# Down projection of a hybrid decoder layer in seven block products, with block sums made in place by POOL and VectorE

## The chip, the cores and the metric

The kernel runs on one core of a Trainium2 chip. The metric is the device time of one execution in microseconds (us). The core's engines run side by side, each through its own queue of instructions in order: TensorE (PE) for matmuls, VectorE (DVE), ScalarE (ACT) and POOL (GpSimd) for elementwise work, and SyncE (SP), whose queue issues most of the DMA transfers here. Semaphores make one engine wait for another. Matmuls write to PSUM, which has eight banks of 128 x 512 float32; everything else lies in SBUF.

## The reference

One layer on 512 tokens of width 1024, all in float32: a mixture of two kinds of attention heads, an output projection onto the residual, then a gated feed-forward part, its down projection onto the residual, and a last RMS norm. Only the end matters here (FFN_HIDDEN is 2816):

```python
def rms_norm(x, g):
    xf = x.astype(jnp.float32)
    y = xf * lax.rsqrt(jnp.mean(xf * xf, axis=-1, keepdims=True) + RMS_EPS)
    return (y * g.astype(jnp.float32)).astype(x.dtype)
...
        h = h + mix @ w_out[layer]
        hn = rms_norm(h, norm2_g[layer])
        h = h + (jax.nn.silu(hn @ w_gate[layer]) * (hn @ w_up[layer])) @ w_down[layer]
    return rms_norm(h, norm_f_g)
```

## The kernel before

A float32 matrix product is made of three matmuls of type float32r: each operand is split into a rounded high part (a copy by ScalarE) and the rest, a low part (a subtraction by VectorE), and high x high, high x low and low x high are added up in PSUM. So every operand costs one ScalarE and one VectorE instruction before TensorE can use it. Line 71 is the helper that copies (`copy`), line 76 the one for two-input operations (`tt`), line 84 the low part in `split`, which attention uses, and lines 95 to 97 (`mm3x`) the three matmuls.

Attention and the output projection fill the first half of the span; there POOL has part of the low parts (line 84) and the scaling of the probabilities (line 337). In the second half the gate and up projections run over 22 blocks (units 0 to 21) of 128 hidden columns each; `first_part`, `second_part` and `third_part` make a unit's seven products and leave its gated hidden block, 128 x 512 (hidden column x token), in `zs[j]`. The normed input lies in X1 (tiles X10, X11) and X2 (X20, X21), high and low parts apart. The last product of a unit (the weight "d", in `third_part`) goes into the same bank A that VectorE has just read for the product before it.

Then comes the down projection, `down_step(k)` for each of 22 row blocks of w_down: SP loads a block (128 x 1024, into a `raw2` tile, six buffers), ScalarE and VectorE split it into an `hl2` tile (three buffers), `split_g` splits the hidden block, and `down` makes 4 token tiles x 2 column halves x 3 matmuls of 512 columns. All eight PSUM banks add up over the 22 blocks. The last four blocks are kept back and done token tile by token tile. As soon as a bank is full, VectorE multiplies it by `nrstd_t` and adds it onto the residual (line 838), which `h1_back` fetched again from DRAM (`h1d`) into `cell(t, c)`; ScalarE squares it with a sum (line 657), `rsqrt` takes the root, and both halves are scaled and stored.

VectorE and ScalarE run `down_step` in the order of the code (`tc.manual_schedule`); all other order, that of TensorE and SP too, is the scheduler's, which may put the first down matmuls between the last gate and up products. A load waits on SP until its buffer is free, and what is behind it on SP waits too.

Of the kernel before, what the change touches and what calls it, by code (L numbers as in the profile page):

```python
# [11 lines left out]
F32 = mybir.dt.float32  # L12
F32R = mybir.dt.float32r
# [3 lines left out]
P = 128  # L17
# [35 lines left out]
def tile_hybrid_layer(ctx: ExitStack, tc: tile.TileContext, xT, w_qk0, w_t, w_av, w_vb, w_o, w_gu, w_d,  # L53
# [605 lines left out]
    def rsqrt(ts, out):  # L659

        v, w, r = nv[:, ts], nt[:, ts], out[:, ts]
        nc.vector.scalar_tensor_tensor(out=v, in0=ss[:, ts, 1], scalar=EPS / 4, in1=ss[:, ts, 0], op0=ALU.add, op1=ALU.add)
        nc.scalar.activation(w, v, AF.Sqrt)
# [78 lines left out]
    def third_part(j, u):  # L742
        y, z = u["y"], zs[j]
        product(u["A"], u["w"]["d"], X2, 4, False)
        tt("v", z[:, :HS], u["A"], y[:, :HS], ALU.mult)
        tt("v", z[:, HS:], z[:, HS:], y[:, HS:], ALU.mult)

    es = []
    for f in range(KT):
# [16 lines left out]
        units[1] = first_part(1)  # L766
    second_norm()
    quads = ["act00", "act01", "act10", "act11"]
    zs = [q[:, i] for tag in quads for q in [act.tile([P, 4, S], F32, name=tag)] for i in range(4)]

    second_part(0, units[0])
    third_part(0, units[0])
    for j in range(1, NJ):
# [7 lines left out]
    GT = [ff.tile([P, n, S], F32R, name=tag, bufs=1) for n, tag in ((4, "X10"), (4, "X11"), (10, "X20"), (10, "X21"))]  # L781
    GH = [GT[0][:, k] for k in range(4)] + [GT[2][:, k] for k in range(10)] + [GT[3][:, k] for k in range(8)]
    GL = [GT[1][:, k] for k in range(4)]
    def w_down(k, w=None):
        raw = raw2()
        nc.sync.dma_start(raw, w_d[k * P:(k + 1) * P, :].rearrange("p (a n) -> p a n", a=2))
        return split2(raw, *ENG["d"], w)

    def split_g(k):
        if k % 4 == 0 and k:  # L790
            q = act.tile([P, 4, S], F32R, name=quads[k // 4 - 1]) if k < 20 else GT[3][:, 8:]
            GL.extend(q[:, i] for i in range(min(4, NJ - k)))
        copy("a", GH[k], zs[k])
        tt("v", GL[k], zs[k], GH[k].bitcast(F32), ALU.subtract)

    def down(ps, t, c, k, w):
        tk = slice(t * P, (t + 1) * P)
        mm3x(ps[c][t], GH[k][:, tk], GL[k][:, tk], w[:, :, c], slice(0, HD), k == 0, k == NJ - 1)

    ps = [[bank(n) for n in ("S", "S", "proj", "proj")], [bank(n) for n in ("PT", "PT", "PT", "O")]]  # L800
    def h1_back(t):
        if t % 2 == 0:
            h1r.append(ff.tile([P, 2, D], F32, name=("X10", "X11")[t // 2], bufs=1))
        nc.sync.dma_start(h1r[t // 2][:, t % 2], h1d[t])

    def cell(t, c):
        return h1r[t // 2][:, t % 2, c * HD:(c + 1) * HD]

    h1r, gf, ws_last, wx = [], [], [], []
    def down_step(k):  # L810
        if k < NJ - LAST:
            w = w_down(k)
        elif k < NJ - 2:
            ws_last.append(w_down(k))
        else:
            if k == NJ - 2:
                wx.append(ff.tile([P, 2, 2, 2, WC], F32R, name="X20", bufs=1))
            ws_last.append(w_down(k, wx[0][:, k - NJ + 2]))
        split_g(k)
        if k < NJ - LAST:  # L820
            for c in range(2):
                for t in range(NT):
                    down(ps, t, c, k, w)
        if k in (1, 2):
            gf.append(ff.tile([P, HD], F32, name="g", bufs=BUFS["g"]))
            nc.sync.dma_start(gf[-1], gf_row[:, (k - 1) * HD:k * HD].to_broadcast([P, HD]))
        if k in (7, 9, 11, 13):
            h1_back((k - 7) // 2)
# [4 lines left out]
    for t in range(NT):  # L833
        for c in range(2):
            for i, k in enumerate(range(NJ - LAST, NJ)):
                down(ps, t, c, k, ws_last[i])
            x = cell(t, c)
            nc.vector.scalar_tensor_tensor(out=x, in0=ps[c][t], scalar=nrstd_t[:, t:t + 1], in1=x, op0=ALU.mult,
                                           op1=ALU.add)
            square(t, c, x)  # L840
            if c == 0:
                tt(ENG["c"], x, x, gf[0], ALU.mult)
        rsqrt(slice(t, t + 1), rstd_t)
# [85 lines left out]
```

## Time and profile before

| | us |
|---|---|
| median of 3 runs (670.36 to 671.63) | 670.62 |
| profiled execution, its own time | 670.29 |
| its span | 668.5 |
| TensorE busy in the span | 641.3 (96%) |
| VectorE busy | 477.3 (71%) |
| ScalarE busy | 352.9 (53%) |
| POOL busy, all of it before 300 us | 144.3 (22%) |
| first down matmul starts | 533.82 |
| last down matmul ends | 661.37 |

The span runs from the first to the last instruction that the profile shows; the time of the execution has a little outside of it. A busy time is a sum over an engine's instructions. An engine with less busy time than span is idle in between, and whether that matters is seen from the chain of waits, which is followed back from the last instruction. Times of the rows are from the start of the span.

### The profile page before, as it was taken

How to read it: one execution, taken by the hardware profiler on the slowest of the kernel's cores; microseconds unless marked ns; L12 is line 12 of the kernel's file. 1: busy time of each engine (PE TensorE's matmuls, PEld its weight loads, DVE VectorE, ACT ScalarE, POOL GpSimd, SP SyncE). 2: the span in 40 equal slices, each digit the busy share in tenths (PEclk: the TensorE clock that was granted, in tenths of full speed). 3: DMA queues.
4: the chain of work that ended last, by engine and by line, in shares of the span. 5: the costliest groups of instructions: out<-in, count | busy, mean ns of one | idle time of the engine just before them, and what ended most of it. 6: DMA issues, size and time to landing. Idle time of an engine off the chain costs nothing.

```text
span 668.5 us, 11164 instructions
## 1 busy us (share of the span) xinstructions
PE 641.3 (96%) x3942; PEld 571.3 (85%) x3942; DVE 477.3 (71%) x994; ACT 352.9 (53%) x745; POOL 144.3 (22%) x184
## 2 busy tenths in 40 slices
PE   9999997999999999987999999999999999999995
PEld 6878887878878887866899999999999988888884
DVE  4458777678787679559899899999998724333355
ACT  5543565345775678558774455545545504222234
POOL 7635842153446645330000000000000000000000
PEclk9999999989999999888899999999999999999998
DMA  6666665446225640063433133323324417222003
GB/s 191 216 177 190 174 176 155 123 140 172 90 95 158 199 150 17 1 206 117 179 128 124 69 111 126 111 95 111 111 96 147 175 58 245 102 94 95 0 2 126
DMA packets 45316, 84.44 MB, mean 126 GB/s; under 512 B 6811, under 2 KB 10139, under 8 KB 45260
## 3 DMA queue, kind: packets, MB, share of 16 engines
q1 hardware_dynamic: 44684, 82.67, 39.1%
q10 hardware_dynamic: 576, 1.05, 0.4%
q8 instruction: 31, 0.51, 0.3%
q14 instruction: 25, 0.20, 0.1%
HBM read 68.45 MB, written 7.64 MB: 114 GB/s over the span
## 4 chain that ended last, share of the span: by engine, by line
PE 78%; DVE 8%; ACT 4%; DMA 4%; issue 3%; SPq 2%; POOL 1%; DVEq 0%; ACTq 0%; POOLq 0%
PE proj L89 8%; PE proj L91 8%; PE proj L90 8%; PE S L90 6%; PE S L89 6%; PE S L91 6%; PE PT L340 3%; PE PT L96 2%; PE PT L95 2%; PE PT L97 2%; PE O L356 2%; PE proj L96 2%; PE proj L95 2%; PE proj L97 2%; PE S L317 2%
## 5 line engine op out<-in xcount | busy, mean ns | idle before, releaser
L76 DVE TENSOR_TENSOR hl<-raw,hl 128x1024 fp32r<-128x1024 f32 x64 | 78.0, 1220 | 61.1 <-ACT hl L71 60.8
L71 ACT CAST hl<-raw 128x1024 fp32r<-128x1024 f32 x64 | 67.3, 1053 | 76.8 <-PE O L97 57.1
L84 POOL TENSOR_TENSOR w_hl<-w_raw,w_hl 128x512 fp32r<-128x512 f32 (+1 forms) x47 | 61.4, 1309 | 61.7 <-ACT w_hl L71 31.5
L71 ACT CAST w_hl<-w_raw 128x512 fp32r<-128x512 f32 (+2 forms) x76 | 43.3, 576 | 58.0 <-PE S L91 18.9
L325 ACT ACTIVATE P<-P,mn 128x512 f32<-128x512 f32 (+1 forms) x96 | 53.5, 559 | 13.3 <-DVE mn L323 13.0
L337 POOL TENSOR_SCALAR P<-P,den 128x512 f32<-128x512 f32 (+1 forms) x96 | 51.4, 554 | 41.4 <-DVE den L329 21.5
L76 DVE TENSOR_TENSOR PTl<-PT,PTh 128x512 fp32r<-128x512 f32 (+2 forms) x96 | 43.7, 482 | 10.2 <-ACT PTh L350 9.9
L323 DVE CUSTOM_DVE_ANT_0 P<-S,T 128x512 f32<-128x512 f32 (+1 forms) x96 | 44.0, 483 | 9.8 <-PE S L318 7.6
L89 PE MATMUL S<-X,hl 128*128 128x256 f32 x176 | 49.9, 284 | 0.7 <-ACT xf L721 0.7
L90 PE MATMUL S<-X,hl 128*128 128x256 f32 x176 | 50.0, 284 | 0.3 <-DVE X L76 0.3
L89 PE MATMUL S<-X,w_hl 128*128 128x256 f32 x176 | 49.7, 284 | 0.5 <-ACT xf L732 0.5
L350 ACT CAST PTh<-PT 128x512 fp32r<-128x512 f32 (+2 forms) x96 | 38.2, 426 | 22.7 <-PE PT L340 18.8
L90 PE MATMUL S<-X,w_hl 128*128 128x256 f32 x176 | 49.8, 283 | 0.0
L91 PE MATMUL S<-X,hl 128*128 128x256 f32 x176 | 49.7, 282 | 0.0
L91 PE MATMUL S<-X,w_hl 128*128 128x256 f32 x176 | 49.7, 283 | 0.0
L89 PE MATMUL proj<-xh,w_hl 128*128 128x512 f32 x112 | 45.6, 408 | 0.5 <-DVE va L282 0.4
L71 ACT CAST w_hl<-raw 128x512 fp32r<-128x512 f32 x45 | 27.3, 619 | 35.5 <-PE S L91 28.3
L90 PE MATMUL proj<-xl,w_hl 128*128 128x512 f32 x112 | 44.7, 399 | 0.0
L91 PE MATMUL proj<-xh,w_hl 128*128 128x512 f32 x112 | 44.6, 398 | 0.0
L84 DVE TENSOR_TENSOR w_hl<-w_raw,w_hl 128x512 fp32r<-128x512 f32 (+1 forms) x37 | 27.4, 747 | 15.7 <-ACT w_hl L71 14.4
L340 PE MATMUL PT<-ident,P 128*128 128x128 f32 x240 | 36.8, 277 | 0.8 <-POOL P L337 0.8
L89 PEld LDWEIGHTS S<-X,hl 128*128 128x128 f32 x176 | 33.9, 193 | 1.1 <-ACT xf L721 1.1
(316 smaller groups left out, 1965.1 us busy)
## 6 DMA issues: line engine op xcount, KB each, us to landing
raw<-in_w_gu_dram SPq DMA_DIRECT2D x46, 256.0 KB, 3.3
raw<-in_w_d_dram SPq DMA_DIRECT2D x22, 512.0 KB, 3.3
w_raw<-in_w_gu_dram SPq DMA_DIRECT2D x42, 256.0 KB, 2.7
w_raw<-in_w_t_dram SPq DMA_DIRECT2D x28, 256.0 KB, 2.8
T<-gd SPq DMA_DIRECT2D x64, 64.0 KB, 1.9
w_raw<-in_w_o_dram SPq DMA_DIRECT2D x16, 256.0 KB, 3.1
w_raw<-in_w_vb_dram SPq DMA_DIRECT2D x16, 140.0 KB, 2.2
Qb<-in_xT_dram SPq DMA_DIRECT2D x8, 256.0 KB, 2.8
```

The lines of the kernel that those rows point to most:

```text
L71: nc.scalar.copy(out, in_)
L76: engines[e].tensor_tensor(out=out, in0=in0, in1=in1, op=op)
L84: engines[lo].tensor_tensor(out=w[:, 1, :n], in0=raw[:, :n], in1=w[:, 0, :n].bitcast(F32), op=ALU.subtract)
L89: nc.tensor.matmul(ps, w[:, 0, sl], xh, start=first, stop=False, skip_group_check=skip)
L90: nc.tensor.matmul(ps, w[:, 0, sl], xl, start=False, stop=False, skip_group_check=skip)
L91: nc.tensor.matmul(ps, w[:, 1, sl], xh, start=False, stop=last, skip_group_check=skip)
L95: nc.tensor.matmul(ps, xh, w[:, 0, sl], start=first, stop=False)
L323: nc.vector.tensor_tensor_reduce(out=pp, in0=sv, in1=T[:, S - w:], op0=ALU.add, op1=ALU.min, scale=1.0, scalar=3e38, accum_out=mn[:, t:t + 1])
L325: nc.scalar.activation(pp, pp, AF.Exp, bias=mn[:, t:t + 1], scale=-1.0, accum_out=den[:, t:t + 1])
L337: nc.gpsimd.tensor_scalar(pp, pp, den[:, t:t + 1], 1.0, op0=ALU.mult, op1=ALU.mult)
L340: nc.tensor.transpose(pv[:, kb * P:(kb + 1) * P], pp[:, kb * P:(kb + 1) * P], ident)
L350: nc.scalar.copy(ov[0], pv)
```

## The change

The hidden activations are seen as a matrix A of 512 tokens x 2816, the weights as a matrix B of 2816 x 1024. Both are cut in two each way: A11, A12 are the first 256 tokens with the first and the second half of the hidden columns, A21, A22 the last 256 tokens; B11 and B12 are the two column halves of w_down's first half of rows, B21 and B22 of the second. A half is 11 row blocks, taken in six steps: five of two blocks and one of a single block. Seven products of such blocks, with sums of blocks as operands, take the place of eight plain ones; a product is 11 row blocks x 2 token tiles x 3 matmuls.

The sums are made in place, a step at a time: s1 to s4 overwrite A11 and A21, t1 to t4 overwrite B11 and B12. POOL makes s1, s4 and t1 to t4, VectorE s2 and s3. They are put into the program three steps ahead of the step that uses them (AHEAD); s1 and s3 go with product 0. The products run one after another. After the third step of the next product, VectorE adds a product's banks onto the residual at the places where its sum is wanted (`evict`), so PSUM keeps adding up from product to product where the same sum goes on. `prepare` splits both operands of a step (tiles xe and xf for the activations, hl2 for the weights), `multiply` makes the matmuls. The order on VectorE, ScalarE, POOL and TensorE is the code's, and SP's as well: B11 into raw2 tiles, B12 into what was X1 and a bit of X2, the residual into X20, B22 into X21, B21 into w_hl tiles, then the gain. Unit 21's last product is moved behind step 0 of the down projection. The last three steps of product 6 are kept back and done one token tile after the other.

```diff
-    third_part(NJ - 1, units[NJ - 1])
...
-    with tc.manual_schedule(engines={mybir.EngineType.DVE, mybir.EngineType.Activation}):
-        for k in range(NJ):
-            down_step(k)
...
+    HJ = NJ // 2
+    PAIRS = [slice(k, min(k + 2, HJ)) for k in range(0, HJ, 2)]
...
+    A11, A12, A21, A22 = [hidden(h, r) for h in range(2) for r in range(2)]
...
+    ps_a, ps_c, ps_b = [[bank(n) for n in tags] for tags in (("PT", "O"), ("S", "S"), ("proj", "proj"))]
...
+    def s1(k):
+        tt("p", A21[k], A21[k], A22[k], ALU.add)
...
+    def s2(k):
+        minus("v", A21[k], A22[k], A11[k])
...
+    def s3(k):
+        minus("v", A11[k], A11[k], A21[k])
...
+    def s4(k):
+        minus("p", A21[k], A12[k], A21[k])
...
+    def t1(k):
+        minus("p", B11[k], B12[k], B11[k])
...
+    def t2(k):
+        minus("p", B11[k], B22[k], B11[k])
...
+    def t3(k):
+        minus("p", B12[k], B22[k], B12[k])
...
+    def t4(k):
+        minus("p", B11[k], B21[k], B11[k])
...
+    def evict(ps, th, c):
...
+        for i in range(2):
+            x = cell(2 * th + i, c)
+            nc.vector.scalar_tensor_tensor(out=x, in0=ps[i], scalar=nrstd_t[:, 2 * th + i:2 * th + i + 1], in1=x,
+                                           op0=ALU.mult, op1=ALU.add)
...
+    products = [
+        (ps_a, A11, B11, True, (), [(ps_a, 0, 0)], []),
+        (ps_c, A21, B11, True, (t1,), [(ps_c, 1, 1)], []),
+        (ps_a, A21, B11, False, (s2, t2), [(ps_a, 0, 1)], []),
+        (ps_c, A21, B22, False, (s4,), [(ps_c, 0, 1)], [(0, 1), (1, 1)]),
+        (ps_a, A11, B12, False, (t3,), [(ps_a, 1, 1)], [(2, 1), (3, 1)]),
+        (ps_b, A12, B21, True, (), [(ps_b, 0, 0)], [(0, 0), (1, 0)]),
+        (ps_a, A22, B11, False, (t4,), [], [])]
+    AHEAD = 3
...
+    def prepare(n, k):
+        a, b = products[n][1][k], products[n][2][k]
+        m = a.shape[1]
+        w = ff.tile([P, 2, 2, WC], F32R, name="hl2", bufs=BUFS["hl2"])
+        gh = ff.tile([P, 2, HS], F32R, name="xe", bufs=BUFS["xe"])
+        gl = ff.tile([P, 2, HS], F32R, name="xf", bufs=BUFS["xf"])
+        copy("a", gh[:, :m], a)
+        minus("v", gl[:, :m], a, gh[:, :m].bitcast(F32))
+        copy("a", w[:, 0, :m], b)
+        minus("v", w[:, 1, :m], b, w[:, 0, :m].bitcast(F32))
+        return gh, gl, w
...
+            parts = prepare(n, k)
+            if x == 2:
+                gated(NJ - 1, units[NJ - 1])
+            if n == 0:
+                s3(k)
+                s1(k)
+            if x + AHEAD < len(steps):
+                m, kk = steps[x + AHEAD]
+                for f in products[m][4]:
+                    f(kk)
...
+            if x == 0:
+                last_product(NJ - 1, units[NJ - 1])
+            if n and k == 2:
+                for e in products[n - 1][5]:
+                    evict(*e)
```

POOL's queue ended with the output projection, long before this part (act are hidden tiles of the attention, mf its output):

```order
L337 TENSOR_SCALAR P<-P,den 128x128
L337 TENSOR_SCALAR P<-P,den 128x256
L372 TENSOR_TENSOR act_446<-mf,act_444 128x512
L84 TENSOR_TENSOR w_hl<-w_raw,w_hl 128x512 x3
L925 UNCONDITIONAL_BRANCH
L925 ISA
```

Now it goes on from there. This is the stretch from the third of s1 to the third of t2 (act and h1t hold the hidden blocks, raw_6445 to raw_6450 B11, X_6462 to X_6464 B12, X_6465 B22; a sum over a pair of row blocks of activations is 128x2x256, of weights 128x1024):

```order
L75 TENSOR_TENSOR act_3771<-act_3771,h1t 128x2x256 x2
L75 TENSOR_TENSOR raw_6445<-X_6462,raw_6445 128x1024
L75 TENSOR_TENSOR act_3772<-act_3772,h1t 128x2x256
L75 TENSOR_TENSOR raw_6446<-X_6462,raw_6446 128x1024
L75 TENSOR_TENSOR act_3772<-act_3772 128x256
L75 TENSOR_TENSOR raw_6447<-X_6463,raw_6447 128x1024
L75 TENSOR_TENSOR raw_6448<-X_6463,raw_6448 128x1024
L75 TENSOR_TENSOR raw_6449<-X_6464,raw_6449 128x1024
L75 TENSOR_TENSOR raw_6450<-raw_6450 128x512
L75 TENSOR_TENSOR raw_6445<-X_6465,raw_6445 128x1024
L75 TENSOR_TENSOR raw_6446<-X_6465,raw_6446 128x1024
L75 TENSOR_TENSOR raw_6447<-X_6465,raw_6447 128x1024
```

36 sums follow the output projection where nothing stood. VectorE had two operations a row block in this part, the low part of the weights (hl) and of the hidden block (here act_6598, the high part in X_6453):

```order
L76 TENSOR_TENSOR hl_6595<-raw_6593,hl_6595 128x1024
L76 TENSOR_TENSOR act_6598<-act_3771,X_6453 128x512
L76 TENSOR_TENSOR hl_6627<-raw_6625,hl_6627 128x1024
L76 TENSOR_TENSOR act_6598<-act_3771,X_6453 128x512
L76 TENSOR_TENSOR hl_6658<-raw_6656,hl_6658 128x1024
L76 TENSOR_TENSOR act_6598<-act_3771,X_6453 128x512
```

Now, in product 1, from its third step to its fifth (xf is the low part of the activations, hl that of the weights, X_6464 holds the residual, act_3770 at the left is s2):

```order
L75 TENSOR_TENSOR xf<-act_3771,xe 128x512
L75 TENSOR_TENSOR hl_6695<-raw_6447,hl_6695 128x1024
L867 SCALAR_TENSOR_TENSOR X_6464<-PT,nrstd_t,X_6464 128x512
L867 SCALAR_TENSOR_TENSOR X_6464<-O,nrstd_t,X_6464 128x512
L75 TENSOR_TENSOR xf<-act_3771,xe 128x512
L75 TENSOR_TENSOR hl_6717<-raw_6448,hl_6717 128x1024
L75 TENSOR_TENSOR act_3770<-act_3773,act_3770 128x2x256
L75 TENSOR_TENSOR xf<-act_3772,xe 128x512
L75 TENSOR_TENSOR hl_6738<-raw_6449,hl_6738 128x1024
```

Two low parts a step are left, on weights of half the width and two row blocks; between them now stand the adds onto the residual (line 867) and s2.

## Rows read from the trace of the kernel before

**Rows 1.** The page: busy us, share of the span, instructions of each engine.

```profile
PE 641.3 (96%) x3942; PEld 571.3 (85%) x3942; DVE 477.3 (71%) x994; ACT 352.9 (53%) x745; POOL 144.3 (22%) x184
```

**Rows 2.** By stage: length, busy us (count) PE PEld DVE ACT POOL, PEclk, DMA.

```profile
560.00:580.00 20.00, 20.00 (x88) 16.19 (x87) 6.86 (x8) 6.27 (x8) 0.00 (x0) 1.00 0.55 193
620.00:640.00 20.00, 20.00 (x87) 16.19 (x87) 8.96 (x10) 7.64 (x10) 0.00 (x0) 1.00 0.00 0
```

**Rows 3.** TensorE's first down matmul, then the chain of waits: start, us, what.

```profile
533.82 0.40 PE L95 MATMUL proj<-hl,X 128*128 128x512 f32 x1
...
556.04 0.70 PE PT L95 x3
...
661.13 0.25 PE O L97
...
661.40 0.76 DVE X L838
```

**Rows 4.** Groups by form, 555 to 650 us: busy us, mean ns, idle before.

```profile
L76 DVE TENSOR_TENSOR hl<-raw,hl 128x1024 fp32r<-128x1024 f32 x16 | 19.6, 1225 | 52.9 <-ACT hl L71 52.8
...
L71 ACT CAST hl<-raw 128x1024 fp32r<-128x1024 f32 x15 | 15.8, 1052 | 57.1 <-PE O L97 57.1
...
L76 DVE TENSOR_TENSOR act<-act,X 128x512 fp32r<-128x512 f32 x12 | 8.2, 684 | 0.0
...
L71 ACT CAST X<-act 128x512 fp32r<-128x512 f32 x11 | 6.8, 614 | 0.0
```

**Rows 5.** Order in time on VectorE: start us, us, line, operation, tiles.

```profile
530.13 0.42 DVE L76 TENSOR_TENSOR g<-PT,xf 128x256 f32<-128x256 f32 x1 [0.54 <-ACT xf L721]
...
539.00 0.42 DVE L76 TENSOR_TENSOR h1t<-S,xf 128x256 f32<-128x256 f32 x1 [1.35 <-PE S L91]
```

**Rows 6.** Order in time on SP: the first loads of w_down.

```profile
509.68 20.26 SPq L786 DMA_DIRECT2D raw<-in_w_d_dram  x7
```

**Rows 7.** Order in time on POOL: two sums without company.

```profile
132.44 1.28 POOL L84 TENSOR_TENSOR w_hl<-w_raw,w_hl 128x512 fp32r<-128x512 f32 x1 [5.69 <-ACT w_hl L71]
133.82 0.61 POOL L462 TENSOR_TENSOR cy<-cy,cmn 128x256 f32<-128x256 f32 x1
```

**Rows 8.** The same form on POOL and VectorE side by side, then VectorE alone.

```profile
144.12 1.46 POOL L84 TENSOR_TENSOR w_hl<-w_raw,w_hl 128x512 fp32r<-128x512 f32 x1
...
144.47 1.66 DVE L84 TENSOR_TENSOR w_hl<-w_raw,w_hl 128x512 fp32r<-128x512 f32 x1
...
158.59 0.69 DVE L84 TENSOR_TENSOR w_hl<-w_raw,w_hl 128x512 fp32r<-128x512 f32 x1
```

**Rows 9.** Four VectorE additions beside three POOL sums, and means by form.

```profile
63.69 1.60 POOL L84 TENSOR_TENSOR w_hl<-w_raw,w_hl 128x512 fp32r<-128x512 f32 x1 [1.08 <-PE proj L402]
66.18 3.19 POOL L84 TENSOR_TENSOR w_hl<-w_raw,w_hl 128x512 fp32r<-128x512 f32 x2 [0.89 <-ACT w_hl L71]
...
63.47 4.74 DVE L387 TENSOR_TENSOR Qb<-pf,pos_sb 64x512 f32<-64x512 f32 x4
...
L387 DVE TENSOR_TENSOR Qb<-pf,pos_sb 64x496 f32<-64x496 f32 x2 | 3.3, 1666 | 0.0
L387 DVE TENSOR_TENSOR Qb<-pf,pos_sb 64x512 f32<-64x512 f32 x2 | 1.4, 682 | 0.0
```

**Rows 10.** A VectorE operation on PSUM under a POOL sum.

```profile
160.44 1.30 POOL L84 TENSOR_TENSOR w_hl<-w_raw,w_hl 128x512 fp32r<-128x512 f32 x1 [2.86 <-PE PT L340]
...
160.62 0.69 DVE L76 TENSOR_TENSOR PTl<-PT,PTh 128x512 fp32r<-128x512 f32 x1 [0.32 <-ACT PTh L350]
```

**Rows 11.** Stretches of 1 us, TensorE alone: busy us (count), PEclk, DMA.

```profile
112.00:113.00 1.00, 0.00 (x0) 1.00 0.38 126
113.00:114.00 1.00, 0.04 (x1) 1.00 0.54 143
...
115.00:116.00 1.00, 1.00 (x3) 0.50 0.39 119
...
118.00:119.00 1.00, 1.00 (x6) 1.00 0.51 170
```

More of the change, by code (lines that the diff above doesn't have):

```diff
@@ L34 @@
 RB = 32
-LAST = 4
 DELAY = 3
@@ L777, in tile_hybrid_layer @@
         second_part(j, units[j])
-    third_part(NJ - 1, units[NJ - 1])
[L781 to L804, printed above, removed]
-    def cell(t, c):
[L807 to L828, printed above, removed]
@@ new lines, in tile_hybrid_layer, with hidden, load_w @@
+    PAIRS = [slice(k, min(k + 2, HJ)) for k in range(0, HJ, 2)]
+    def hidden(half, rows):
+        v = []
+        for k in PAIRS:
+            j = k.start + (NJ - 10 if k.start < 10 else 1) * rows
+            v.append(zq[min(j // 4, 4)][:, j - 4 * min(j // 4, 4):][:, :k.stop - k.start, half * HS:(half + 1) * HS])
+        return v
+    A11, A12, A21, A22 = [hidden(h, r) for h in range(2) for r in range(2)]
+    def load_w(dst, kh, ch):
+        for n, k in enumerate(PAIRS):
+            for i in range(k.stop - k.start):
+                r = k.start + i + ((NJ - 10 if k.start < 10 else 1) if kh else 0)
+                nc.sync.dma_start(dst[n][:, i], w_d[r * P:(r + 1) * P, ch * HD:(ch + 1) * HD])
@@ new lines, in minus @@
+    def minus(e, out, in0, in1):
+        tt(e, out, in0, in1, ALU.subtract)
+    ps_a, ps_c, ps_b = [[bank(n) for n in tags] for tags in (("PT", "O"), ("S", "S"), ("proj", "proj"))]
+    def cell(t, c):
+        return x0[2][:, 2 * t + c]
+    with tc.manual_schedule(engines={mybir.EngineType.SP}):
+        r11 = [raw2() for _ in PAIRS]
+        B11 = r11[:5] + [r11[5][:, 0:1]]
+        load_w(B11, 0, 0)
+        x0 = [ff.tile([P, n, WC], F32, name=tag, bufs=1)
+              for n, tag in ((4, "X10"), (4, "X11"), (10, "X20"), (10, "X21"))]
+        B12 = [x0[k // 2][:, 2 * (k % 2):2 * (k % 2) + 2] for k in range(4)] + [x0[2][:, 8:10], r11[5][:, 1:2]]
+        load_w(B12, 0, 1)
+        for t in range(NT):
+            nc.sync.dma_start(x0[2][:, 2 * t:2 * t + 2], h1d[t].rearrange("p (c n) -> p c n", c=2))
+        B22 = [x0[3][:, 2 * k:2 * k + 2] for k in range(5)] + [raw1()[:, None]]
+        load_w(B22, 1, 1)
+        B21 = [ws.tile([P, 2, WC], F32, name="w_hl", bufs=BUFS["w_hl"]) for _ in range(5)] + [raw1()[:, None]]
+        load_w(B21, 1, 0)
+        gf = [ff.tile([P, HD], F32, name="g", bufs=BUFS["g"]) for _ in range(2)]
+        for c in range(2):
+            nc.sync.dma_start(gf[c], gf_row[:, c * HD:(c + 1) * HD].to_broadcast([P, HD]))
@@ new lines, in tile_hybrid_layer @@
+    AHEAD = 3
+    steps = [(n, k) for n in range(7) for k in range(len(PAIRS))]
+    def prepare(n, k):
[9 more added lines that the diff above has]
+        return gh, gl, w
@@ new lines, in multiply @@
+    def multiply(n, i, k, gh, gl, w):
+        ps, first = products[n][0], products[n][3]
+        s = slice(i * P, (i + 1) * P)
+        for j in range(PAIRS[k].stop - PAIRS[k].start):
+            start, stop = first and k == 0 and j == 0, PAIRS[k].start + j == HJ - 1
+            nc.tensor.matmul(ps[i], gh[:, j, s], w[:, 0, j], start=start, stop=False, skip_group_check=True)
+            nc.tensor.matmul(ps[i], gh[:, j, s], w[:, 1, j], start=False, stop=False, skip_group_check=True)
+            nc.tensor.matmul(ps[i], gl[:, j, s], w[:, 0, j], start=False, stop=stop, skip_group_check=True)
@@ new lines, in tile_hybrid_layer @@
+    last = []
+    with tc.manual_schedule(engines={mybir.EngineType.DVE, mybir.EngineType.Activation, mybir.EngineType.Pool,
+                                 mybir.EngineType.PE}):
+        for x, (n, k) in enumerate(steps):
+            if x == len(PAIRS):
+                nc.scalar.activation(nt[:, 0:1], ones[:, 0:1], AF.Sqrt)
+            parts = prepare(n, k)
[8 more added lines that the diff above has]
+                    f(kk)
+            if n == 6 and k >= 3:
+                last.append((k, *parts))
+            else:
+                for i in range(2):
+                    multiply(n, i, k, *parts)
+            if x == 0:
[3 more added lines that the diff above has]
+                    evict(*e)
+            if n and k == 3:
+                for c in products[n - 1][6]:
+                    close(*c)
@@ new lines, in final @@
+    def final(i):
+        x = cell(2 + i, 0)
+        nc.vector.scalar_tensor_tensor(out=x, in0=ps_a[i], scalar=nrstd_t[:, 2 + i:3 + i], in1=x, op0=ALU.mult,
+                                       op1=ALU.add)
+    r2, r3 = slice(2, 3), slice(3, 4)
+    with tc.manual_schedule(engines={mybir.EngineType.DVE, mybir.EngineType.Activation, mybir.EngineType.PE}):
+        root(slice(0, 2))
+        unroot(slice(0, 2))
+        for t in range(2):
+            scale(t)
+            store(t)
+        for x in last:
+            multiply(6, 0, *x)
+        final(0)
+        close(2, 0)
+        root(r2)
+        for x in last:
+            multiply(6, 1, *x)
+        unroot(r2)
+        scale(2)
+        final(1)
+        square(3, 0, cell(3, 0))
+        store(2)
+        root(r3)
+        gain(3)
+        unroot(r3)
+        scale(3)
+        store(3)
```

47 lines of the change are left out of this document (27 added, 20 removed).

## The prediction

> **What bounds the kernel now.** I read the engines' busy times first, then a table by stage, then the chain of waits, then single instructions where engines meet. TensorE is busy for 96% of the span, VectorE for 71%, POOL for 22% [rows 1]. The stage that the change rewrites begins with the first down matmul at 533.82, in between the last gate and up matmuls, and its last matmul ends at 661.37, where the chain passes to VectorE [rows 3]. The table says which engine is short there: TensorE 20.00 of 20.00 us at granted clock 1.00, VectorE 6.86 to 8.96, ScalarE 6.27 to 7.64, POOL nothing [rows 2]. So here a matmul saved is time saved, as long as the other engines keep up. Three matmuls take 0.70 in the chain, 0.233 each [rows 3]. 22 row blocks of 24 matmuls are 528, or 123.2 us; of the 127.55 us from 533.82 to 661.37 the other 4.35 are gate and up matmuls. After TensorE come 7.1 us of closing work up to the end of the span at 668.5, and the profiled execution took 670.29, so 1.8 us lie outside the span; its time is 0.33 under the median of 670.62, less than the runs differ.
>
> **TensorE's share of the change.** Seven products of 11 row blocks, 2 token tiles and 3 matmuls are 462, which is 66 fewer: 66 x 0.233 = 15.4 us. A full step (two row blocks) has 12 matmuls, 2.80 us, the sixth step of a product 1.40, a product 15.4. The last gate and up product now stands between steps 0 and 1 with nothing to fill its wait for VectorE's read of the same bank (the add took 0.42 [rows 5]); I take 0.8, between 0 and 1.5. Alone, this gives a TensorE end of 661.4 - 15.4 + 0.8 = 646.8.
>
> **Splits, loads, evictions.** A full step now splits two row blocks of half width and its own activations: ScalarE 0.61 + 1.05, VectorE 0.68 + 1.23 [rows 4], some 1.7 and 1.9 against 2.80. Each is covered if nothing delays it; three weight buffers (hl2) let a split run at most two steps ahead. The 14 adds onto the residual take 0.76 each [rows 3] and come two in a step. The loads are as many bytes as before. B11 goes into the buffers that took the first w_down blocks before, seven of them issued from 509.68 on [rows 6]; the others wait on SP for X1 and X2 to be free, with only loads queued behind, and POOL wants B22 and B21 tens of us later. I cost them at nothing; if a load is late, it is a us or two. The closing chain is the same operations, 7.1 us.
>
> **The sums on POOL.** Before, POOL did nothing in this stage. Now it has 12 activation sums (s1, s4) and 24 weight sums (t1 to t4). Two inputs of 128x512 took 1.28, of 128x256 0.61 [rows 7]; 128x1024 does not occur. Twice 1.28 is 2.56, and 1.28 plus two more steps of 0.67 is 2.62; I take 2.6, bounds 2.45 and 2.75. POOL's total is 4 x (5 x 2.6 + 1.28) = 57.1 and 2 x (5 x 1.28 + 0.61) = 14.0, together 71 us. Alone that would fit beside 107.8 us of matmuls.
>
> **But the two engines exclude each other.** A VectorE split of 128x512, both inputs in SBUF, takes 0.69 when POOL is idle; begun at 144.47 beside a POOL sum of 144.12 to 145.58 it took 1.66 and ended at 146.13, 0.55 after POOL did [rows 8]. So it did not slow down, it stood still. [Rows 9] show who goes next: four VectorE additions in a row, while POOL had three sums to do. Two took 682 ns, two 1666; the four took 4.74, which is 4 x 0.54 + 2 x 1.28 = 4.72, and POOL's sums ended as if each had gone in after one VectorE operation. They take strict turns, each for a whole operation. A VectorE operation with one input in PSUM runs through: 0.69 under a POOL sum [rows 10]. So the residual adds don't take part, and all splits and the sums s2 and s3 do. The Trainium skill has the rule that speaks against this change: SBUF — State Buffer, section Who interferes with whom, says that a VectorE instruction with two SBUF inputs contends with a GpSimd one that reads SBUF, and the later one fully blocks. The trace agrees on that and on its exemption of one SBUF input; without the exemption the 14 adds would put some 10 us more into the shared time, with it nothing.
>
> **The ledger of the shared access.** A VectorE operation holds it for 0.54 (128x512), 1.22 - 0.14 = 1.08 (128x1024) or 0.28 (128x256). The turns make POOL's work and VectorE's add up until POOL's last sum, t4 of step 5. By when does that come? t4 waits behind t3 and s4 in POOL's queue, and s4 overwrites A21 only after product 2's splits have read it. So t3 and t4, 12 sums, fall beside product 3's 12 splits, one for one. VectorE's holds through product 3: 4 products x (5 x 1.62 + 0.82) = 35.7, s2 and s3 2 x 2.98 = 6.0, leftovers of units 20 and 21 1.6, sum 43.3. With POOL's 71 that is 114. It starts near 530.6, when s3 of step 0 can go behind the read of PT at 530.13 [rows 5]; that gives 645, and I add 4 for stretches in which neither can work (VectorE's queue stands behind the last gate and up product until 541.8): 649. Seen by step: a full step of product 3, and most of product 1, has two sums and two splits in turn, 2 x 2.6 + 1.62 = 6.8 us where TensorE needs 2.80. TensorE, the bound before, starves.
>
> After 649 VectorE is alone and TensorE the bound again: 1.4 for product 3's last step and its split, 3 x 15.4 = 46.2 for products 4 to 6, and 2 for refilling the queue of prepared steps: 699. Starving also costs clock: after TensorE had stood still from 112 to 114 the granted clock was 0.50 (1.2 GHz) for some 3 us and then 1.00 again [rows 11]. In a starved step 2 x 2.80 = 5.6 still fits under 6.8, so I add only 2: 701. With 7.1 and 1.8 the time is **710 us**, 6% slower.
>
> **Rivals.**
> *The sums do not collide (faster).* If POOL's sums found the gaps in VectorE's queue, or these forms did not exclude each other, TensorE would end at 646.8 plus 1 for the tight last steps, and the time is 647.8 + 7.1 + 1.8 = 657. For it: POOL's results are wanted late, and VectorE has some 1 us free per step. Against: that gap is shorter than one sum of 2.6, and every meeting of such a pair in rows 8 and 9 shows the wait. It decides if a split beside a sum takes under about 1.6. With half-collisions up to 669.
> *Exclusive, but better packed.* The shared work in all is 71 + 7 x 8.9 + 6.0 + 5 (gains, stores, leftovers) = 144. If VectorE's late splits could fill every gap, it would end at 530.6 + 144 = 675, with 4 of matmuls, 7.1 and 1.8 behind: 688. Sums of 2.45 in place of 2.6 save 3. For it: turns need not be strict where both are ready at once. Against: hl2's three buffers keep VectorE from splitting ahead of TensorE in products 4 to 6. 688 to 703.
> *The clock stays low.* If TensorE stays at the half level through the starved products, product 2, whose steps have only some 3.8 us of shared work, is paced by 5.6: 5 x 1.8 = 9 more, and a stretch at half level in product 4 costs 2 more: 720. The Trainium skill's TensorE: Matmul & The Clock Gate, section HAM oscillation, tells of a kernel that fell back to the low rate at every step's wait; [rows 11] agree on the fall and show it end after some 3 us. Sums of 2.75 would add 3. 718 to 730.
> *The change does not do what it says*: the order of the instructions has the 462 matmuls in place of 528 and all 36 sums, so no chance is kept for this.
>
> **How the numbers follow.** Turns as computed, 703 to 718: 0.66, since rows 8 to 10 fit to 0.1 us and what is uncertain is the time in which neither works. Better packed: 0.12. Clock or longer sums: 0.11. No collision, or little: 0.10. No difference to be seen: 0.01. A measurement of this kernel tells about 0.2% from no change; by that bound faster is 0.10, same 0.01, slower 0.89. The range reaches to 695 and 724, which takes in both bounds of the 2.6, most of the packed case and half of the clock case.
>
> **What would show it.** In the profile after, POOL's 128x1024 sums should read 3 to 3.7 us rather than 2.6, and VectorE's 128x1024 splits beside them up to 3.7 rather than 1.23; both should fall back to their own times after POOL's last sum, near 649. TensorE should take some 36 us for products 1 and 3, some 20 for product 2, and 15.4 to 16 for products 4 and 5. The time between the last matmul and the end should again be 7 us. The prediction is wrong if VectorE's splits keep 1.23 under POOL's sums (then 657), if POOL has finished before product 2 begins, or if products 4 to 6 are not back at 15.4, in which case something else, a load or the clock, bounds them.

## The result, and the profile after

The changed kernel took 698.16 us (median of 4 runs, 696.08 to 698.63), the kernel before 671.12 in the same comparison: a ratio of 1.0393, interval 1.0362 to 1.0424. It is 27 us slower, where the forecast was 710 with a range of 695 to 724. The profiled execution took 698.63 with a span of 696.8, so again 1.8 us lie outside the span.

The page of the changed kernel, first the busy us of each engine (beside [rows 1]), then the rows of 40 slices, in tenths:

```profile
PE 640.2 (92%) x3876; PEld 565.9 (81%) x3876; DVE 574.3 (82%) x1049; ACT 380.2 (55%) x785; POOL 231.7 (33%) x220
...
PE   8999998899999999888999999999999866867995
...
POOL 6525842345354655200000000000001697797000
PEclk9999998999999999998999999999999988977998
```

TensorE has 66 instructions fewer, VectorE 55 more and POOL 36 more. In the last ten slices TensorE's row falls to 6 to 8 where POOL's row is 6 to 9, and recovers when POOL stops (the last slice is the closing work).

The table by stage (length, busy us of PE, PEld, DVE, ACT, POOL with counts, granted clock, DMA share, GB/s), beside [rows 2]. The stretches are about those of product 1, product 2, product 3, product 4 and product 5:

```profile
555.00:588.00 33.00, 20.88 (x70) 15.02 (x69) 33.00 (x19) 10.27 (x14) 29.91 (x12) 0.84 0.42 154
589.00:608.00 19.00, 16.14 (x62) 12.69 (x63) 19.00 (x19) 7.53 (x11) 12.79 (x7) 0.91 0.00 0
609.00:643.00 34.00, 22.36 (x63) 16.06 (x63) 34.00 (x16) 8.18 (x12) 31.52 (x12) 0.75 0.00 1
643.80:658.80 15.00, 15.00 (x68) 12.42 (x67) 11.09 (x15) 9.65 (x16) 0.00 (x0) 1.00 0.01 1
658.80:673.70 14.90, 14.90 (x67) 12.34 (x66) 11.23 (x15) 9.81 (x17) 0.00 (x0) 1.00 0.00 0
```

In product 3 VectorE shows 34.00 busy of 34.00 with 16 instructions, in product 4 only 11.09 of 15.00 with 15. So beside POOL a VectorE instruction "is busy" for 2.1 us on average, without it for 0.74. The order in time on VectorE and POOL (start, us, engine, line, operation) shows how:

```profile
611.16 2.87 DVE L75 TENSOR_TENSOR xf<-act,xe 128x512 fp32r<-128x512 f32 x1
613.94 3.39 DVE L75 TENSOR_TENSOR hl<-X,hl 128x1024 fp32r<-128x1024 f32 x1
617.26 2.88 DVE L75 TENSOR_TENSOR xf<-act,xe 128x512 fp32r<-128x512 f32 x1
620.06 3.38 DVE L75 TENSOR_TENSOR hl<-X,hl 128x1024 fp32r<-128x1024 f32 x1
623.36 0.74 DVE L867 SCALAR_TENSOR_TENSOR X<-PT,nrstd_t,X 128x512 f32<-128x512 f32 x1
...
640.99 0.68 DVE L75 TENSOR_TENSOR xf<-act,xe 128x512 fp32r<-128x512 f32 x1
641.59 1.21 DVE L75 TENSOR_TENSOR hl<-X,hl 128x1024 fp32r<-128x1024 f32 x1
```

```profile
607.32 15.03 POOL L75 TENSOR_TENSOR X<-X,X 128x1024 f32<-128x1024 f32 x5
622.31 2.26 POOL L75 TENSOR_TENSOR raw<-w_raw,raw 128x512 f32<-128x512 f32 x1
624.54 14.55 POOL L75 TENSOR_TENSOR raw<-w_hl,raw 128x1024 f32<-128x1024 f32 x5
639.05 1.47 POOL L75 TENSOR_TENSOR raw<-w_raw,raw 128x512 f32<-128x512 f32 x1
```

The splits, 0.68 and 1.21 after POOL's last sum ended at 640.52, read 2.87 and 3.39 before it. From the start of one split to the start of the next it is 2.78 and 3.32: less VectorE's own holds of 0.54 and 1.08 the same 2.24 both times. That is one POOL sum in every turn, and not a slowing in proportion, which would lengthen the longer split by more. The add onto the residual at 623.36, which has an input in PSUM, takes 0.74 in the midst of it. A full step is 613.94 to 620.06, 6.12 us.

### The profile page after: what moved, and what is told of

Same layout as the page of the kernel before. It is cut to its first block, busy times and chain, and to the rows that moved or that the text cites. A ratio compares the mean times of both kernels' runs of the same rounds, so it can differ in the third digit from the quotient of the medians.

```text
span 696.8 us, 11223 instructions
## 1 busy us (share of the span) xinstructions
PE 640.2 (92%) x3876; PEld 565.9 (81%) x3876; DVE 574.3 (82%) x1049; ACT 380.2 (55%) x785; POOL 231.7 (33%) x220
## 4 chain that ended last, share of the span: by engine, by line
PE 68%; DVE 21%; issue 4%; ACT 3%; DMA 2%; POOL 0%; SPq 0%; ACTq 0%; DVEq 0%; POOLq 0%
PE proj L88 8%; PE proj L90 8%; PE proj L89 8%; PE S L88 6%; DVE hl L75 6%; PE S L89 6%; PE S L90 6%; DVE xf L75 5%; PE PT L339 3%; DVE act L75 2%; PE PT L88 2%; PE PT L89 2%; PE PT L90 2%; PE O L355 2%; PE S L316 2%
## 5 line engine op out<-in xcount | busy, mean ns | idle before, releaser
L75 DVE TENSOR_TENSOR hl<-raw,hl 128x1024 fp32r<-128x1024 f32 (+1 forms) x69 | 91.2, 1324 | 5.2 <-ACT hl L70 5.2
L70 ACT CAST hl<-raw 128x1024 fp32r<-128x1024 f32 (+1 forms) x69 | 70.4, 1021 | 41.9 <-PE O L920 13.0
L75 POOL TENSOR_TENSOR act<-act,act 128x512 f32<-128x512 f32 x4 | 7.5, 1870 | 239.3 <-DVE act L75 237.4
L70 ACT CAST w_hl<-w_raw 128x512 fp32r<-128x512 f32 (+2 forms) x76 | 43.3, 577 | 59.8 <-PE S L90 18.8
L75 DVE TENSOR_TENSOR xf<-act,xe 128x512 fp32r<-128x512 f32 (+1 forms) x36 | 48.1, 1336 | 0.3 <-ACT xe L70 0.3
L88 PE MATMUL proj<-xh,w_hl 128*128 128x512 f32 x112 | 46.2, 412 | 0.0
L919 PE MATMUL S<-hl,xe 128*128 128x512 f32 x44 | 22.7, 516 | 23.8 <-DVE hl L75 23.8
```

The costliest lines, as they stand in the source:

```text
L70: nc.scalar.copy(out, in_)
L75: engines[e].tensor_tensor(out=out, in0=in0, in1=in1, op=op)
L88: nc.tensor.matmul(ps, w[:, 0, sl], xh, start=first, stop=False, skip_group_check=skip)
L919: nc.tensor.matmul(ps[i], gh[:, j, s], w[:, 1, j], start=False, stop=False, skip_group_check=True)
```

## The experiments

The theory (turns): POOL's sums and VectorE's operations with two SBUF inputs exclude each other, each for a whole operation. The rivals: late results (POOL's sums are simply slow, and the splits wait for their results), and the clock or the loads.

**POOL without reading.** Each of the 36 sums became two memsets of the same tile, for instance

```diff
-        minus("p", B12[k], B22[k], B12[k])
+        nc.gpsimd.memset(B12[k], 0.01)
+        nc.gpsimd.memset(B12[k], 0.02)
```

> The changed kernel with each of POOL's 36 sums replaced by two memsets of the same tile: POOL stays busy for a comparable time in the same places of its queue and the same instructions wait for it, but it reads nothing. The products then multiply constants where the sums would stand, so the output is another. Turns theory (POOL's sums and VectorE's operations with two inputs in SBUF exclude each other): VectorE's splits fall back to 0.68 and 1.22 beside POOL's work, TensorE ends at about 647 to 650, closing 8.0 and 1.8 outside the span, time 656 to 662. Rival, late results (a split waits because POOL's own work takes long, not because of exclusion): POOL's chain is nearly as long as before, so 685 to 698. Rival, clock or loads: nothing is changed about either, 695 to 700.

Measured: 655.44 us, 0.976 of before (0.9734 to 0.9786). Groups by form of this kernel, POOL and then VectorE (busy us, mean ns, idle before):

```profile
L862 POOL MEMSET X<- 128x1024 f32 x5 | 4.8, 958 | 0.0
L863 POOL MEMSET X<- 128x1024 f32 x5 | 4.8, 958 | 0.3
...
L75 DVE TENSOR_TENSOR hl<-X,hl 128x1024 fp32r<-128x1024 f32 x10 | 12.2, 1222 | 5.9 <-ACT hl L70 5.9
```

POOL is as good as fully busy (9.71 us of 10 between 590 and 600), and the splits keep 1222 ns. Products 1 to 6 take 15.0 us each, and the changed kernel loses 42.7 us to this run. Two memsets take 1.9 us (2 x 0.958) where a sum alone takes 2.40, so POOL's chain is a little shorter here; the next run keeps its length. The Trainium skill, SBUF — State Buffer, section Who interferes with whom, says that a VectorE instruction with two SBUF inputs does not contend with a GpSimd one that only writes; the trace agrees, 1222 ns beside the memsets and 1225 before [rows 4].

**POOL with one input.** The same with one operation that reads and writes the tile:

```diff
-        minus("p", B12[k], B22[k], B12[k])
+        nc.gpsimd.tensor_scalar(B12[k], B12[k], 0.5, None, op0=ALU.mult)
```

> The changed kernel with each of POOL's 36 sums replaced by one POOL operation with one SBUF input (the same tile times 0.5, in place), so the output is another. It tells what of POOL's operation excludes VectorE's: if any POOL operation that reads SBUF does, VectorE's splits beside it wait for it as a whole and the time is 670 to 698, by how long such an operation takes (its own duration is in no trace so far); if two inputs are needed for it, or exclusion has nothing to do with it, the splits keep 0.68 and 1.22 and the time is 654 to 658, as with the memsets.

Measured: 661.71 us, 0.9862 (0.9838 to 0.9885): between the two cases. Groups by form:

```profile
L858 POOL TENSOR_SCALAR X<-X 128x1024 f32<-128x1024 f32 x5 | 15.8, 3178 | 0.0
L852 POOL TENSOR_SCALAR raw<-raw 128x1024 f32<-128x1024 f32 x5 | 14.7, 2944 | 0.0
...
L75 DVE TENSOR_TENSOR xf<-act,xe 128x512 fp32r<-128x512 f32 x28 | 26.1, 933 | 0.7 <-ACT xe L70 0.7
L75 DVE TENSOR_TENSOR hl<-X,hl 128x1024 fp32r<-128x1024 f32 x10 | 13.3, 1329 | 1.0 <-ACT hl L70 1.0
```

This refutes late results: POOL's operations last 2.9 to 3.2 us, as the sums did in the changed kernel (2.9 to 3.1), and the same instructions wait for them, yet the time is 36 us less. It also shows that reading alone does not lock VectorE out for the whole operation: over the whole stage a split loses 0.1 to 0.25 us on average. The averages hide how. In order of time, a POOL operation and VectorE beside it:

```profile
572.67 3.21 POOL L855 TENSOR_SCALAR raw<-raw 128x1024 f32<-128x1024 f32 x1
```

```profile
573.18 1.52 DVE L75 TENSOR_TENSOR xf<-act,xe 128x512 fp32r<-128x512 f32 x1
574.62 1.21 DVE L75 TENSOR_TENSOR hl<-raw,hl 128x1024 fp32r<-128x1024 f32 x1
575.75 0.68 DVE L75 TENSOR_TENSOR act<-h1t,act 128x512 f32<-128x512 f32 x1
```

Under one POOL operation of 3.21 us the first VectorE operation begun beside it reads 1.52 instead of 0.68, 0.84 more, and the ones after it keep their own times. It is so with each of the four POOL operations from 566.26 to 579.07; elsewhere one cost as much, less or nothing. So it holds the access for up to 0.84, where a sum of two tiles held it for 2.24.

**The collision put into the kernel before.** Sums on a free tile that nobody reads, from the first split on:

```diff
+            if k == 0:
+                for _ in range(40):
+                    nc.gpsimd.tensor_tensor(out=x, in0=x, in1=x, op=ALU.subtract)
```

> The kernel before, with 40 sums of 128x1024 put on POOL from the first split of the down stage on (a free tile minus itself), whose result nobody reads, so no instruction waits for one. Turns theory: VectorE's two splits of a row block (holds of 0.54 and 1.08) alternate with two sums of about 2.25: 6.1 us for a block where TensorE needs 5.6, so over 20 blocks TensorE falls behind by up to 10 us, less the lead of the prepared blocks: 676 to 681; each sum reads 3 to 3.5 us, VectorE's 128x1024 split about 3.4. Rival, late results: nothing waits for these sums, so 669 to 672. Rival, both engines slow each other down in proportion to what they move: as in the next run, whatever it is.

Measured: 674.11, 1.0053 (1.0034 to 1.0072). With half the size, 80 times:

> The same with 80 sums of 128x512 in place of 40 of 128x1024: the same elements, half the size of a turn. Turns theory: two turns of about 1.14 and 1.62 of VectorE's own make 3.9 us for a block, under TensorE's 5.6, so nothing is lost on the path: 669 to 673. Rival, slowing down in proportion: the same elements are summed, so the same time as with 40 sums of 128x1024. Rival, late results: 669 to 672 in both.

Measured: 671.03, 1.0000 (0.9988 to 1.0012). The order (large pieces cost, small ones don't) is as the turns have it, and not as a slowing in proportion to the elements summed, which are as many in both; but the first was expected at 676 to 681. Its splits read 2.38 and 2.91 and a block took 5.14 us, under TensorE's 5.6, so it hardly shows; it loses about 3 us between 540 and 550 (TensorE busy for 7.01 of 10.00), where VectorE's gate and up operations took turns too. In this run a sum held the access for only (5.14 - 1.62) / 2 = 1.76. The difference to the changed kernel's sums is that it reads one tile twice, so the next run reads two (in0=y):

> The run with 40 sums of 128x1024 on POOL beside the kernel before, but with two different input tiles, as t1 to t4 have them. In the run before this one the sums took a tile minus itself; turns were seen (splits of 2.38 and 2.91), but one sum held the access for only (5.14 - 1.62) / 2 = 1.76, so a block took 5.14, under TensorE's 5.6, and the time rose by 3 us only. Turns theory: with the 2.25 that a sum held in the changed kernel a block takes 6.1, above 5.6: splits read 2.9 and 3.4, TensorE falls behind by 0.5 a block and waits in nearly every one, time 677 to 684. If the price of a turn is not set by the inputs, 672 to 675 as before. Rival, late results: 669 to 672.

Measured: 688.00, 1.0247 (1.0216 to 1.0279). VectorE in order of time, first of the run with one tile, then of that with two:

```profile
574.02 2.91 DVE L76 TENSOR_TENSOR hl<-raw,hl 128x1024 fp32r<-128x1024 f32 x1
576.85 2.38 DVE L76 TENSOR_TENSOR act<-act,X 128x512 fp32r<-128x512 f32 x1
```

```profile
582.57 3.42 DVE L76 TENSOR_TENSOR hl<-raw,hl 128x1024 fp32r<-128x1024 f32 x1
585.91 2.89 DVE L76 TENSOR_TENSOR act<-act,X 128x512 fp32r<-128x512 f32 x1
588.72 3.42 DVE L76 TENSOR_TENSOR hl<-raw,hl 128x1024 fp32r<-128x1024 f32 x1
```

A block is 582.57 to 588.72, 6.15 us, to 0.05 what the turns give, and above 5.6. So 40 unneeded sums cost a kernel 16 us in which nothing waits for their results. The time came out above the 677 to 684 expected. I had counted only the 0.5 us per block, but the row of the stretch from 540 to 550 has TensorE busy for 4.54 of 10.00 us while VectorE's last gate and up operations, which TensorE needs there, stand between the same sums:

```profile
540.00:550.00 10.00, 4.54 (x12) 3.33 (x11) 8.10 (x5) 0.30 (x1) 9.77 (x4) 0.77 0.27 79
```

**Part of the sums on VectorE.** t3 and t4 alone (`"p"` becomes `"v"` in these two lines):

> The changed kernel with the 12 sums t3 and t4 on VectorE instead of POOL, the other 24 on POOL. No split of product 3 needs t3 or t4. Turns theory: these sums are what slows product 3 from 15 to 35.0 us; it falls to 15 to 20 us, products 0 to 2 stay as they are (TensorE's product 1 at 32 to 33 us), products 5 and 6 have 0.6 us of VectorE work more per step and stay at about 15; time 678 to 686. Rival, late results: product 3 waits for s4 and its own splits, which stay on POOL and VectorE, so product 3 stays at 30 us or more and the time is 694 to 700, or more by VectorE's 12 added operations.

Measured: 682.88, 1.0177 (1.0153 to 1.0202). Product 3 falls from 35.0 us to 15.2 (first matmuls at 609.38 and 624.59), product 1 stays at 32.4. Then all 36 sums on VectorE:

> The changed kernel with all 36 sums on VectorE, POOL idle in the down projection. VectorE by its own durations without POOL beside it: splits 7 x (5 x (0.68 + 1.22) + 1.1) = 74.2, weight sums 4 x (5 x 1.22 + 0.68) = 27.1, activation sums 4 x 3.75 = 15.0, 14 adds of 0.76 = 10.6, gains 2.8: 130 us from 530.6, against 105 us of matmuls. Turns theory: VectorE is the bound, but no operation waits for a turn: TensorE ends at 660 to 664, time 669 to 674, 24 to 29 us faster than the changed kernel and level with the kernel before. Rival, late results (VectorE is short of time as it is and needs POOL's help): 34.6 us more work on VectorE makes it 700 to 730. Rival, clock or loads: 695 to 700.

Measured: 669.38, 0.9972 (0.9959 to 0.9984): 29 us faster than with POOL's help. VectorE is now the bound by its own work, as two stretches in products 1 and 2 show (columns as above):

```profile
570.00:580.00 10.00, 7.77 (x32) 5.80 (x33) 10.00 (x13) 4.91 (x6) 0.00 (x0) 1.00 0.16 58
590.00:600.00 10.00, 9.47 (x42) 7.85 (x43) 10.00 (x15) 5.36 (x8) 0.00 (x0) 1.00 0.01 2
```

**Sums without either engine.** If VectorE is full and POOL is in its way, the queues can add: ScalarE negates the block, a transfer issued by POOL adds the other one onto it. s1 and s4 go to VectorE.

```diff
-        minus("p", B11[k], B22[k], B11[k])
+        nc.scalar.activation(B11[k], B11[k], AF.Copy, scale=-1.0)
+        nc.gpsimd.dma_start(B11[k], B22[k], accum_op=ALU.add)
```

> The changed kernel with the activation sums s1 and s4 on VectorE and the weight sums made by the DMA queues: ScalarE negates the block in place (24 times about 1.05 us) and a transfer issued by POOL adds the other block onto it. No POOL instruction then reads SBUF; VectorE has 103 us of work and ScalarE some 90 against 105 of matmuls. Turns theory: TensorE is the bound again if a transfer's sum is there within the 8 us by which it is ordered ahead: TensorE ends at 647 to 655, time 657 to 665, faster than both kernels. If an accumulating transfer of 512 KB takes more than 2.8 us of the queues or lands later than 8 us, 670 to 720. Rival, clock: no better than 690.

Measured: 666.57, 0.9938 (0.9913 to 0.9962), faster than both kernels but not 657 to 665. Products 3 to 6 take 15.0 to 15.5 us, products 1 and 2 20.5 and 22.5. The waits between 550 and 600 (who for whom: us, times, longest), and the transfers' median us from issue to landing between 540 and 600:

```profile
ACT hl L70 <- DMA raw<-X: 15.6, 9, 3.9
...
raw<-X POOLq DMA_DIRECT2D x10, 512.0 KB, 8.2
```

There the queues also carry the loads. So t1 went to VectorE, and the loads of B21, not needed before product 5, to ScalarE's queue in product 2 (in step 15: `load_w(B21, 1, 0, nc.scalar)`).

> The kernel with the weight sums made by accumulating transfers, changed in two places after its trace: t1 goes to VectorE, and the loads of B21 are issued by ScalarE in product 2 (step 3) rather than behind those of B22. In the run before, ScalarE's copies waited 15.6 us for accumulating transfers between 550 and 600, where the queues were full (share over 1.0) and a transfer of 512 KB took 8.2 us to land; products 1 and 2 took 20.5 and 22.5 us, the later ones 15.0. Theory: the queues were short in these two products; with 2.9 MB of accumulation and 2.75 MB of loads out of that stretch, product 1 takes 17 to 19 (VectorE has 19 us of work in it) and product 2 15 to 18: 658 to 664. Rival, the latency of one accumulating transfer is what counts, not the load on the queues: product 2 stays at 20 or more, 664 to 667.

Measured: 665.41, 0.992 (0.9902 to 0.9939). Product 1 took 18.9, product 2 20.0. The rival's number came out, for another reason: ScalarE stood in issuing the loads, in order of time

```profile
578.46 6.72 ACTq L809 DMA_DIRECT2D w_hl<-in_w_d_dram  x10
585.53 0.33 ACTq L809 DMA_DIRECT2D w_raw<-in_w_d_dram  x1
585.90 0.62 ACT L70 CAST xe<-act 128x512 fp32r<-128x512 f32 x1 [6.42 <-DMA w_hl<-in_w_d_dram]
```

Spread over the six steps of product 3 (`if 18 <= x < 24`, two row blocks in each step but the last):

> The kernel with t2 to t4 made by accumulating transfers and t1 on VectorE, with the loads of B21 issued by ScalarE two at a time in the six steps of product 3. In the run before, ScalarE's sequencer stood 7.1 us in issuing the eleven loads while the queues were full of accumulation, and TensorE waited 3.7 us in product 2 for it. Theory: in product 3 the queues are empty at first, so an issue costs ScalarE little; product 2 takes 15 to 16.5 instead of 20.0 us, time 659 to 663. Rival: issuing costs ScalarE 0.64 us a load wherever it is; two in a step of 2.72 beside 1.66 of copies and 1.05 of negation delay product 3 by 1.3 us a step, time 664 to 668.

Measured: 660.27 us, 0.9835 (0.9813 to 0.9857), 11 us faster than the kernel before and 38 than the changed one. Products 2 to 6 take 15.0 to 15.4 us. The loads in product 3 landed in 4.4 us (median), and TensorE is busy throughout:

```profile
580.00:590.00 10.00, 10.00 (x46) 8.26 (x45) 9.71 (x14) 6.55 (x9) 0.00 (x0) 1.00 0.38 107
590.00:600.00 10.00, 10.00 (x46) 8.29 (x45) 9.01 (x13) 7.57 (x11) 2.58 (x3) 1.00 0.82 214
```

So the seven products are worth having; it was where the sums were made that was not.

**Two details of the forecast.** The last gate and up product put back ahead of step 0, where it stood before:

> The changed kernel with the last gate and up product before step 0 of the down products, as it stood before the change, instead of between steps 0 and 1. The prediction took the move to cost 0.8 us of stall, 0 to 1.5. Turns theory: step 0 stands later and the stall moves ahead of it, but products 1 to 3 are set by the shared work of VectorE and POOL, which starts with s3 and s1 of step 0 and not with its matmuls, so the time is 697 to 700, the same within 1.5 us. Rival (the move matters, since VectorE's queue stands behind that product until 542): 694 to 696.

Measured: 698.41, 1.041 (1.0378 to 1.0441), the same as the changed kernel. TensorE idles for 1.97 us between 530 and 550 instead of 0.52, so the move saves 1.45 there; the shared work of VectorE and POOL swallows it. And the order of the matmuls in a step, with the bank changed after every 3:

```diff
-                for i in range(2):
-                    multiply(n, i, k, *parts)
+                for j in range(2):
+                    for i in range(2):
+                        multiply(n, i, k, *parts, blocks=(j,))
```

> The changed kernel with the matmuls of a step in another order: row block outside, token tile inside, so that TensorE changes its bank after every 3 matmuls, as the kernel before did, and not after 6. It tells why a down matmul takes 0.227 us after the change (products 4 to 6: 14.95 us for 66) and took 0.233 before. If a change of bank has a price, products 4 to 6 go back to 15.4 us each and the time rises by 1 to 1.5 us; if not, they stay at 14.95 and the time within 1 us of the changed kernel's 698.2, since products 0 to 3 wait for VectorE and POOL.

Measured: 699.62, 1.0423 (1.0398 to 1.0449). Product 4 took 15.35, product 5 14.96. One at 14.96 with four changes of bank in a step, where the changed kernel has two, means that these have no price; the 0.4 of product 4 stands where the prepared steps begin to fill again. Why a matmul takes 0.227 us here and 0.233 before stays open.

## Why the prediction was right, and where its sizes were off

The forecast was 710. Its main case, 703 to 718, missed the 698.16 by 5 us; the range held because it also took in most of a rival. The mechanism was right, the main price in it was not.

**The bound and the outside.** The lost time is where the prediction put it: TensorE starves in products 1 and 3, which took 32.5 us (555.95 to 588.42, first matmul to first matmul) and 35.0 (608.76 to 643.78) where 36 each were forecast; product 2 took 20.3 (some 20), products 4 and 5 15.0 (15.4 to 16). The 1.8 outside the span held.

**Mutual exclusion in strict turns**, read from three waits in the kernel before ([rows 8], [rows 9]), held for the pairs in product 3, and so did the exemption of the residual adds ([rows 10]; 0.74 at 623.36). The splits' 3.39 is within the "up to 3.7", the POOL sum's 3.0 (15.03 / 5) and 2.9 (14.55 / 5) at the lower edge of the "3 to 3.7" and just under it.

**The price of a POOL sum was the term that failed.** I took 2.6 for 128x1024 with bounds of 2.45 and 2.75; alone it takes 2.40, as the run with unneeded sums on two tiles shows in a stretch where VectorE is idle:

```profile
L841 POOL TENSOR_TENSOR h1t<-h1t 128x1024 f32<-128x1024 f32 x5 | 12.0, 2403 | 0.4
```

and it holds the access for 2.24. Two mistakes went the same way: I carried the step from 128x256 to 128x512 on in proportion, and I took VectorE's holds as its durations less 0.14 but POOL's as its full durations. 2 x (1.28 - 0.14) = 2.28 would have been 0.04 from it. With 2.24, 1.14 and 0.5 for the three sizes the ledger's POOL part is 4 x (5 x 2.24 + 1.14) + 2 x (5 x 1.14 + 0.5) = 61.8 instead of 71; with VectorE's 43.3, the start at 530.6 and the 4 of idle time it ends at 639.7. Measured: 640.5, forecast 649. The rest of the ledger was right to 1 us as a sum, in part by luck: the 43.3 has the 1.6 of step 0's splits in it, which ran before 530.6, and the stretches in which neither engine worked came to 5.2 instead of 4. The Trainium skill's GPSIMD Engine Reference, section Elementwise — side-by-side cycle accounting, lists 4497 ns for an addition of 2048 fp32 elements a partition; half of it, 2.25 as an estimate, would have been nearer to the 2.40 measured alone than my 2.6.

**After POOL.** POOL's last sum ended 8.5 us before the forecast's 649, but product 4 began at 643.78, only 6.6 before the forecast's 650.4: 3.3 us after that sum, where I had 1.4. The clock is in this. After standing still from 634 to 636 (busy 0.00) TensorE made the last two steps of product 3 at the lower level (1.2 GHz). In the run with the gate and up product put back it had 2.4 GHz there, and product 4 began 1.9 after POOL's last sum (640.29 to 642.17). The same stretch of the changed kernel and of that run:

```profile
638.00:640.00 2.00, 2.00 (x6) 1.59 (x5) 2.00 (x2) 0.00 (x0) 2.00 (x2) 0.50 0.00 0
```

```profile
638.00:640.00 2.00, 1.69 (x8) 1.07 (x6) 2.00 (x2) 0.45 (x1) 2.00 (x2) 1.00 0.00 0
```

From 643.8 on the clock read 1.00, and 198 matmuls took 45.05 to TensorE's end at 688.8, where I had 46.2, 2 for refilling and 2 for the clock. The 1.15 less is the 0.227 for 0.233 of a matmul. Refilling cost nothing to be seen here (product 4 took 14.97) and 0.4 in the run with the higher clock (15.32), so from POOL's last sum to TensorE's end it was 48.3 us here and 47.3 there: as an estimate, the clock cost 1 us of the 2 put in for it. Inside products 1 and 3, where matmuls started 0.43 apart in places, as around 569, the turns set the pace. Together 6.6 + 1.15 + 4 and 0.4 of rounding are the 12.2 between 701 and 688.8.

**The closing** took 8.0, not 7.1 ([rows 3] have the 661.37 it was taken from). The operations are not in the same order: ScalarE still scales token tile 2 and issues its store, when the last add has ended,

```profile
689.05 0.72 ACT L880 ACTIVATE X<-X,rstd_t 128x512 f32<-128x512 f32 x1 [0.74 <-DVE rstd_t L672]
689.80 0.34 ACTq L881 DMA_DIRECT2D out_dram<-X  x1
690.18 0.63 ACT L656 ACTIVATE g<-X 128x512 f32<-128x512 f32 x1 [0.41 <-ACT X L880]
```

so the square begins 0.52 after the last add ended at 689.66 (0.08 before), and the gain of tile 3 stands between the sum of squares and its reciprocal, which comes 0.68 after that sum instead of 0.42. 0.44 and 0.26 are most of the 0.9. 688.8 + 8.0 + 1.8 = 698.6 is the profiled execution's 698.63.

**The move of the last gate and up product** was costed at 0.8, between 0 and 1.5: the stall is 0.5, and the run with it undone showed that it does not reach the end. **Loads** cost a 0.36 wait of POOL, as forecast about nothing. **Splits** have their own times as soon as POOL is quiet.

**The rivals.** No collision was priced at 657; the run with memsets took 655.4, so the price was right and the condition didn't hold. The better packed case had 688 to 703, and the time fell into that bracket, but not by packing: VectorE and POOL did take strict turns, and the sums were shorter than the 2.45 that I had given this rival as its end. The clock case, 9 us and more on top of the 2, did not occur.

## What to carry to other kernels

Work that is moved to an idle engine is only free if the two engines don't take turns at something: price it as the sum of both engines' holds in the stretch, not as the longer of the two. Here VectorE alone with all the sums (an estimated 130 us of its own work) beat VectorE with POOL's help by 29 us, since a POOL sum held the access for 2.24 where VectorE would have needed 1.08. If an operation must go there, look for a form that doesn't collide, or for a shorter time (a write, an accumulating transfer, one input), and keep the pieces so small that two turns fit under the consumer's pace: on one tile 80 sums of 128x512 cost nothing where 40 of 128x1024 cost 3 us. With two tiles the 40 cost 16 us; halves of these were not run.

## What the runs showed of the hardware that was not expected

- A POOL sum of a 128x1024 tile with itself held VectorE off for 1.76 us, one of two tiles for 2.24, though both wrote the same. Why is open.
- A POOL operation with one SBUF input lasted 2.9 to 3.2 us and held VectorE off once, for up to 0.84 (1.52 instead of 0.68), so it does not exclude the splits for its whole length. Why is open, as is its length: with a constant as factor 128x512 took 1.7 us, while line 337 of the kernel before, with a factor for each partition, took 0.70.
- A transfer that adds 512 KB onto SBUF took 8.2 us from issue to landing beside loads, and 6.8 in products 3 and 4 of the fastest version. In a stretch of that version (570 to 580) with hardly anything else in the queues they were full (share 1.02) at 189 GB/s, where loads alone had 391 at a share of 1.04:

```profile
550.00:560.00 10.00, 7.62 (x27) 5.49 (x26) 9.93 (x15) 4.80 (x7) 0.00 (x0) 0.86 1.04 391
...
570.00:580.00 10.00, 10.00 (x45) 8.27 (x45) 10.00 (x15) 8.44 (x11) 2.58 (x3) 1.00 1.02 189
```

- ScalarE's sequencer stood for 6.72 us in issuing ten loads in a row while the queues were full (share 1.01), 0.67 each; spread over product 3, four of the five pairs took 0.82 to 0.87 and one 1.36, and TensorE waited for none. Whether the row of ten or the full queues made the difference was not separated.
- The down matmuls of the changed kernel start 0.227 us apart, those of the kernel before 0.233, both at a granted clock of 1.00. The bank order is not the reason.
